# Cross products of split scores: the low part of q padded with zero rows to 128

## Chip, cores, metric

The kernel runs on one core of a Trainium2 chip. The metric is the device time of one execution in microseconds (us); the median over the runs is quoted. A difference of about 0.3% (some 1.1 us) is the least that a measurement of this kernel can tell from none.

## What is computed

One decoder layer on 256 tokens of width 1024, followed by a last RMS normalisation. Cut to its skeleton:

```python
x = x + hybrid_mixer(rmsnorm(x, g_mix), w_in, g_group, sinks, w_out, rel_table)
x = x + memory_cross_attention(rmsnorm(x, g_cross), rmsnorm(mem, g_mem), w_xq, w_xkv, w_xo)
x = x + squared_relu_mlp(rmsnorm(x, g_mlp), w_up, w_down)
return rmsnorm(x, g_final)
```

The mixer has four groups of four heads of width 64: `a` dilated attention, `b` stick-breaking attention, `c` grouped-query attention with a window and sinks, `d` block attention. The cross-attention has four heads of width 64 over 256 memory tokens. In each of the five a block of scores is q k^T with a contraction over 64, in float32:

```python
s = jnp.einsum("bhqe,bhke->bhqk", q, k) * SCALE + bias
```

## The kernel before

**Precision.** Every large product is made of float32r parts. A matrix is split into a high part (ACT rounds it while copying, L313 for weights) and a low part (DVE subtracts, L314). `mm3` (L418 to L422) adds three products: high by high, high by low, low by high. All three contract over 128 rows.

**Work and its order.** Weights stream through SP's queue in halves of 512 KB into 4 `raw` buffers (L299), and are split into 15 `w` buffers (L313, L314). The code records operations in a `Plan` with a price each; `arrange` makes a list schedule of them by the longest way to the end, and the result is one fixed order of instructions for each engine. The order is thus settled before the kernel runs, and each engine works its own queue from front to back. The stages run: loads and normalisation (to about 17 us of the trace), projections of the four groups with the attention of the group before between them (to about 104 us), output projection of the mixer, cross-attention (about 142 to 168 us), MLP, final normalisation.

**Scores.** For the first 128 queries of a mixer group, the scores are plain float32 products over 64 rows (L629). For the second 128 queries of each group, and for both blocks of the cross-attention, they are float32r products made by `stacked` (L597 to L601). `stack_k` puts for each head the high part of k into the head's own 64 rows of `ks`, and the low part into the other 64. `stack_q` puts the high part of q into both halves of `qs`, and the low part into `ql`, 64 rows for each head. So the first product of `stacked` contracts over all 128 rows (high q with both parts of k), the second over the 64 rows of the head (low q with the high part of k). Each has 128 weight columns and 256 moving columns. `attend` calls `stacked` four times for each mixer group, the cross-attention (L782 to L786) four times for each of its two blocks: 24 pairs, 48 products. By the order of PE's instructions the 48 stand in five runs of eight (groups `a`, `b`, `d`, and both blocks of the cross-attention) and two runs of four (group `c`, one run for each half).

**What stands around a run.** In front of it ACT writes `qs` (L592) and DVE writes `ql` (L593). Behind it, in a mixer group, DVE adds the bias and takes the extremum (L665; L649 in group `b`), ACT takes the exponential (L669), PE transposes the weights (L535), DVE or ACT copies them out of PSUM (L242, L243), and PE multiplies by v (L553). In the cross-attention the reduction is L788 and the exponential L793. On POOL stand the memsets of constants and of the ones in v (L345, L477, L358), the reciprocal roots `rstd` (L383), and some DMAs on its own queue.

Of the kernel before, what the change touches and what calls it, by code (L numbers as in the profile page):

```python
# [18 lines left out]
P = 128  # L19
# [23 lines left out]
def _constants():  # L43
    """One-hot of minus the bucket of each distance, and the additive mask of each bias row.
    Column u stands for the distance u - 127. Rows 0-3 dilated, 4-7 window, 8-11 causal, 12 strictly past."""
    d = np.arange(STRIP) - 127
    n = np.maximum(d, 0)
    nf = np.maximum(n, 1).astype(np.float32)
    large = 16 + (np.log(nf / np.float32(16)) / np.float32(math.log(2048 / 16)) * np.float32(16)).astype(np.int32)
    bucket = np.where(n < 16, n, np.minimum(large, 31))  # L50
    onehot = np.zeros((32, STRIP), np.float32)
    cols = np.arange(STRIP)[d >= 0]
    onehot[bucket[cols], cols] = -1.0
    cnt = ((d >= 0) & (d <= 128)).astype(np.int64) + ((d >= 0) & (d % 4 == 0)) + ((d >= 0) & (d % 16 == 0))
    mask = np.zeros((NROW, STRIP), np.float32)
    mask[0:4] = np.where(cnt > 0, -np.log(np.maximum(cnt, 1)), BIG)
    mask[4:8] = np.where((d >= 0) & (d < 128), 0.0, BIG)
    mask[8:12] = np.where(d >= 0, 0.0, BIG)
    mask[12] = np.where(d > 0, 0.0, BIG)
    return onehot, mask  # L60


class Buf:
    """A tile that is taken from its pool when the first operation on it is issued."""

# [20 lines left out]
class Plan:  # L86
    """Records operations with what they read and write, and issues them in the order of a list schedule:
    of the operations that can start when an engine gets free, the one with the longest way to the end."""

# [125 lines left out]
def trunk(ctx: ExitStack, tc: tile.TileContext, a: dict, out: bass.AP):  # L215
# [16 lines left out]

# [1 line left out]
    def act(n, fn, r, w, aps=0):  # L234
# [5 lines left out]
    def copy(n, out_, in_, r, w):  # L240
        """A copy out of PSUM, by whichever engine is free first."""
        plan.add("DVE", 0.065 + n * 1.05e-3, lambda: nc.vector.tensor_copy(out_(), in_()), r, w,  # L242
                 ("ACT", 0.02 + n * 0.00093, lambda: nc.scalar.activation(out_(), in_(), AF.Copy)))  # L243
# [10 lines left out]
    def dma_late(nbytes, fn, r, w):  # L254
        """On the queue of GpSimd."""
        plan.add("POOL", 1.0, fn, r, w)
        plan.add("DMA", max(0.06, nbytes / 360e3), None, [], w)
# [11 lines left out]

# [1 line left out]
    w_in, w_out = a["w_in"][0], a["w_out"][0]  # L271
# [20 lines left out]
    def load(u, *which):  # L292
        """Fetches and splits halves of a unit."""
        n, c = units[u].shape[1] // 2, units[u].shape[2]
        got = parts.setdefault(u, ([], n))[0]
        for part in which or range(2):
            raw = buf("raw", [P, n, c], F32, RAW)
            hi, lo = buf("w", [P, n, c], F32R, SPL), buf("w", [P, n, c], F32R, SPL)
            dma(n * c * 512, lambda raw=raw, part=part: nc.sync.dma_start(raw.t, units[u][:, part * n:(part + 1) * n]), [], [raw])  # L299
            if u == "cq":  # L300
                def view(z, r):
                    return z.t[:, :, tsl(r)].rearrange("p k (g e) -> p k g e", g=2)

                def src(z, r):
                    return z.t.rearrange("p k (g r e) -> p k r g e", g=2, r=2)[:, :, r]

                for r in range(2):
                    act(512, lambda raw=raw, hi=hi, r=r: nc.scalar.activation(view(hi, r), src(raw, r), AF.Copy),
                        [raw], [(hi, r)])
                    dve(512, lambda raw=raw, hi=hi, lo=lo, r=r: nc.vector.tensor_sub(  # L310
                        view(lo, r), src(raw, r), view(hi, r).bitcast(F32)), [raw, (hi, r)], [(lo, r)])
            else:
                act(1024, lambda raw=raw, hi=hi: nc.scalar.activation(hi.t, raw.t, AF.Copy), [raw], [hi])  # L313
                dve(1024, lambda raw=raw, hi=hi, lo=lo: nc.vector.tensor_sub(lo.t, raw.t, hi.t.bitcast(F32)), [raw, hi], [lo])  # L314
            got.append((hi, lo))

    def wt(u, k):
        """Row block k of a unit: the two buffers and the block's place in them."""
        got, n = parts[u]
        return got[k // n], k % n  # L320

# [1 line left out]
    xt = []  # L323
# [36 lines left out]
    def warm_up(n):  # L360
        """Products of nothing, so that the array's clock is up when the first ones come."""
        wps = acct()
# [15 lines left out]

# [1 line left out]
    def rstd_of(ssq, n):  # L380
# [18 lines left out]
    def transpose(dst, src, view, n, keys):  # L399
        """n blocks of 128 columns of view(), transposed side by side into dst."""  # L400
        def go():
# [4 lines left out]
    def gained_T(x, g, hl, t):  # L406
        """The transposed rows of x, times the gain, split: (t, half of the blocks) at a time."""
        tmp = buf("tmp", [P, KB, P], F32, 3)
# [20 lines left out]
    def proj_T(dst, view, u, i, hT):  # L429
        """view()[c, t] = sum_k w[k, c] hT[k, t]"""  # L430
        for k in range(KB):
# [4 lines left out]
    def proj(dst, view, u, hT, t):  # L436
        """view()[t, c] = sum_k hT[k, t] w[k, c]"""
        for k in range(KB):
# [3 lines left out]

# [1 line left out]
    h1 = pair("hT", KB, 2)  # L444
# [15 lines left out]

# [1 line left out]
    bias = {gi: buf("w", [P, 4, S], F32, SPL) for gi in (0, 2, 3)}  # L462
# [7 lines left out]

# [1 line left out]
    def project(gi):  # L472
# [45 lines left out]

# [1 line left out]
    def own(h):  # L520
# [5 lines left out]
    def transpose_probs(w, t):  # L526
        """w [t, 4, s] -> per head the blocks [s, t], each with its buffer."""
        res = []
# [14 lines left out]
    def weigh(pT, v, kv, vkeys):  # L543
        """Weighted values and their sums: [t, 4, 65]."""
        py = pst()
# [24 lines left out]

    # ---- scores of 128 queries and 256 keys by float32r products: a head's two parts of k above each other in the
    #      rows of the array, met by the high part of q twice; then the low part of q with the high part of k ----
    def rows_of(half):
        return slice(half * E, half * E + E)

    def stack_k(k, view, n):
        """Slot 2 i + half: the high part of the head's rows, and in the other rows their low part."""
        ks = buf("ks", [P, 4, S], F32R, 1)
# [7 lines left out]
    def stack_q(q, view):  # L586
        """The high part twice, above each other, and the low part in its own rows."""
        qs, ql = buf("qs", [P, 4, P], F32R, 1), buf("ql", [P, 2, P], F32R, 1)
        for half in range(2):
            own, other, at = rows_of(half), rows_of(1 - half), slice(half, 4, 2)  # L590
            for r in (own, other):
                act(256, lambda r=r, own=own, at=at: nc.scalar.activation(qs[r, at, :], view()[own], AF.Copy), [q], [(qs, half)])  # L592
            dve(256, lambda own=own, at=at: nc.vector.tensor_sub(  # L593
                ql[own, :, :], view()[own], qs[own, at, :].bitcast(F32)), [q, (qs, half)], [(ql, half)])
        return qs, ql

    def stacked(dst, q, i, ks, j):  # L597
        qs, ql = q
        own = rows_of(i % 2)
        nc.tensor.matmul(dst, qs[:, i, :], ks[:, j, :], start=True, stop=False)  # L600
        nc.tensor.matmul(dst, ql[own, i // 2, :], ks[own, j, :], start=False, stop=True)  # L601

# [92 lines left out]
    def rows_mm(acc, hl, u, t, c0, c1, first, last):  # L695
        """acc += columns c0 to c1 of the sum over the two row blocks of a unit"""
        for j in range(2):
# [30 lines left out]

# [1 line left out]
    mT = pair("hT", KB, 2)  # L730
# [4 lines left out]

# [1 line left out]
    pacc = [[acct() for n in range(2)] for t in range(2)]  # L737
# [8 lines left out]

# [1 line left out]
    pk = pst()  # L748
# [8 lines left out]

# [1 line left out]
    def residual(acc, t, r=None):  # L759
# [51 lines left out]
    plan.fixed = MLP_RANK  # L811
# [1 line left out]
    pieces = [[(acct(), 0, 512), (acct(), 512, D)], [(acct(), 0, 512), (acct(), 512, LASTC), (pst(), LASTC, D)]]  # L813
# [3 lines left out]
    def up_rows(i, hid, t):  # L817
        """Two blocks of hidden features for one block of tokens alone."""
        pu = pst()
# [106 lines left out]
```

## Time and profile before

| | us |
|---|---|
| median of three runs | 361.29 |
| lowest, highest run | 360.21, 361.37 |
| span of the profiled execution, first to last instruction | 357.2 |
| PE busy | 347.0 |
| DVE busy | 230.7 |
| ACT busy | 194.1 |
| POOL busy | 24.9 |

The profiled execution's own device time is not listed beside its span; the median of the runs lies 4.1 us above the span, for what is outside the first and the last instruction. PE is TensorE's products, PEld its weight loads, DVE VectorE, ACT ScalarE, POOL GpSimd, SP the engine whose queue issues most DMAs. The start of a product and the start of the next one tell what it holds the array for; the duration that a row prints for a product is longer, since products are pipelined.

### The profile page before, as it was taken

The numbers are of one execution on the slowest core, as the hardware profiler recorded it, in microseconds if no ns is written. First come the engines' busy times: TensorE is split into PE (matmuls) and PEld (weight loads), VectorE is DVE, ScalarE is ACT, GpSimd is POOL, SyncE is SP. The second block draws the span as 40 slices with busy tenths as digits, with TensorE's granted clock in tenths as the row PEclk, the third lists the DMA queues.
The fourth block names the chain that finished last, engine by engine and source line by source line (L and its number), as shares of the span: only waits on it lengthen the run. The fifth ranks groups of instructions, "written<-read, shape, count | busy, mean of one in ns | idle before, by whom it ended". The sixth has DMA issues, their size and how long they took to land.

```text
span 357.2 us, 6139 instructions
## 1 busy us (share of the span) xinstructions
PE 347.0 (97%) x2442; PEld 316.9 (89%) x2442; DVE 230.7 (65%) x370; ACT 194.1 (54%) x313; POOL 24.9 (7%) x44
## 2 busy tenths in 40 slices
PE   7899999999999999999999999999999999999992
PEld 6798999989888889878999999999999999999982
DVE  3857779579886699668946445464555545465254
ACT  6577677377873467684654435354353534535132
POOL 5430100000201005000010000000000000000000
PEclk9999999999999999999999999999999999999998
DMA  8998574640245335825375555655466554653003
GB/s 247 357 348 254 140 217 124 229 119 0 65 167 182 120 118 159 260 65 167 103 252 178 176 163 192 219 181 192 137 218 195 185 200 135 229 190 107 2 0 117
DMA packets 39900, 59.88 MB, mean 168 GB/s; under 512 B 2006, under 2 KB 33040, under 8 KB 39872
## 3 DMA queue, kind: packets, MB, share of 16 engines
q1 hardware_dynamic: 39216, 57.69, 50.3%
q0 software_dynamic: 640, 1.80, 1.7%
q8 instruction: 19, 0.31, 0.3%
q14 instruction: 9, 0.07, 0.1%
q10 hardware_dynamic: 16, 0.00, 0.0%
HBM read 58.42 MB, written 1.07 MB: 167 GB/s over the span
## 4 chain that ended last, share of the span: by engine, by line
PE 91%; DVE 2%; issue 2%; DMA 2%; POOL 1%; ACT 0%; SPq 0%; POOLq 0%; DVEq 0%
PE acc L420 15%; PE acc L421 15%; PE acc L422 15%; PE ps L421 11%; PE ps L420 11%; PE ps L422 11%; PE ps L553 4%; PE ps L403 3%; PE ps L601 2%; PE ps L600 2%; PE ps L535 2%; DMA x<-in_x_dram 2%; POOL rstd L383 1%; PE ps L629 1%; DVE hTlo L397 1%
## 5 line engine op out<-in xcount | busy, mean ns | idle before, releaser
L314 DVE TENSOR_TENSOR w<-raw,w 128x1024 fp32r<-128x1024 f32 x100 | 120.3, 1220 | 83.4 <-ACT w L313 80.0
L313 ACT ACTIVATE w<-raw 128x1024 fp32r<-128x1024 f32 x100 | 103.4, 1054 | 93.7 <-PE ps L421 43.5
L421 PE MATMUL ps<-hTlo,w 128*128 128x256 f32 x256 | 72.2, 282 | 0.0
L420 PE MATMUL ps<-hThi,w 128*128 128x256 f32 x256 | 72.0, 281 | 0.0
L422 PE MATMUL ps<-hThi,w 128*128 128x256 f32 x256 | 71.8, 280 | 0.0
L420 PE MATMUL acc<-w,yThi 128*128 128x512 f32 (+1 forms) x168 | 64.1, 381 | 0.0
L421 PE MATMUL acc<-w,yThi 128*128 128x512 f32 (+1 forms) x168 | 63.0, 375 | 0.0
L422 PE MATMUL acc<-w,yTlo 128*128 128x512 f32 (+1 forms) x168 | 62.5, 372 | 0.0
L422 PEld LDWEIGHTS ps<-hThi,w 128*128 128x128 f32 x256 | 48.4, 189 | 0.0
L420 PEld LDWEIGHTS ps<-hThi,w 128*128 128x128 f32 x256 | 48.2, 188 | 0.1
L421 PEld LDWEIGHTS ps<-hTlo,w 128*128 128x128 f32 x256 | 48.1, 188 | 0.1
L422 PEld LDWEIGHTS acc<-w,yTlo 128*128 128x128 f32 x168 | 31.5, 188 | 6.1
L420 PE MATMUL acc<-hThi,w 128*128 128x256 f32 x128 | 36.6, 286 | 0.0
L420 PEld LDWEIGHTS acc<-w,yThi 128*128 128x128 f32 x168 | 31.6, 188 | 5.7
L421 PEld LDWEIGHTS acc<-w,yThi 128*128 128x128 f32 x168 | 31.7, 189 | 5.2
L421 PE MATMUL acc<-hTlo,w 128*128 128x256 f32 x128 | 36.1, 282 | 0.0
L422 PE MATMUL acc<-hThi,w 128*128 128x256 f32 x128 | 36.0, 281 | 0.0
L383 POOL TENSOR_TENSOR rstd<-var,mhalf 128x1 f32<-128x1 f32 x16 | 14.9, 932 | 149.6 <-DVE var L382 102.8
L420 PEld LDWEIGHTS acc<-hThi,w 128*128 128x128 f32 x128 | 24.1, 188 | 0.5
L422 PEld LDWEIGHTS acc<-hThi,w 128*128 128x128 f32 x128 | 24.2, 189 | 0.1
L421 PEld LDWEIGHTS acc<-hTlo,w 128*128 128x128 f32 x128 | 24.1, 188 | 0.0
L830 ACT ACTIVATE q<-ps 128x512 f32<-128x512 f32 x15 | 9.0, 599 | 11.8 <-PE ps L422 11.8
(151 smaller groups left out, 523.6 us busy)
## 6 DMA issues: line engine op xcount, KB each, us to landing
raw<-in_w_up_dram SPq DMA_DIRECT2D x32, 512.0 KB, 3.8
raw<-in_w_down_dram SPq DMA_DIRECT2D x32, 512.0 KB, 3.8
raw<-in_w_in_dram SPq DMA_DIRECT2D x22, 512.0 KB, 4.9
raw<-in_w_out_dram SPq DMA_DIRECT2D x8, 512.0 KB, 3.4
raw<-in_w_xkv_dram SPq DMA_DIRECT2D x4, 512.0 KB, 3.7
w<-dstrip POOLq DMA_DIRECT2D x3, 512.0 KB, 8.3
x<-in_x_dram SPq DMA_DIRECT2D x2, 512.0 KB, 6.0
tmp<-in_mem_dram SPq DMA_DIRECT2D x2, 512.0 KB, 5.8
```

The lines of the kernel that those rows point to most:

```text
L313: act(1024, lambda raw=raw, hi=hi: nc.scalar.activation(hi.t, raw.t, AF.Copy), [raw], [hi])
L314: dve(1024, lambda raw=raw, hi=hi, lo=lo: nc.vector.tensor_sub(lo.t, raw.t, hi.t.bitcast(F32)), [raw, hi], [lo])
L383: pool(0.5, lambda: nc.gpsimd.tensor_tensor(r.t, v.t, mhalf.t, op=ALU.pow), [v, mhalf], [r])
L403: nc.tensor.transpose(dst[:, tsl(k)], view()[:, tsl(k)], ident.t)
L420: nc.tensor.matmul(dst, lh, rh, start=start, stop=False)
L421: nc.tensor.matmul(dst, lh, rl, start=False, stop=False)
L422: nc.tensor.matmul(dst, ll, rh, start=False, stop=stop)
L535: nc.tensor.transpose(pt[:, tsl(i)], w[:, h, tsl(j)], ident.t)
L553: nc.tensor.matmul(view()[:, h, :], z[:, i, :], v[:, j, kv(h), :], start=j == 0, stop=j == len(pT[h]) - 1)
L600: nc.tensor.matmul(dst, qs[:, i, :], ks[:, j, :], start=True, stop=False)
L601: nc.tensor.matmul(dst, ql[own, i // 2, :], ks[own, j, :], start=False, stop=True)
L830: act(512, lambda: nc.scalar.activation(r.t, pu.t.rearrange("p (i t) -> p i t", i=2), AF.Relu), [pu], [r])
```

## The change

`ql` becomes two buffers of 128 rows and four slots, made once and zeroed by POOL at the start. Calls of `stack_q` take them in turn. The low part of a head goes into its own 64 rows of its own slot; the other 64 rows of the slot stay zero. The second product of `stacked` takes the whole slot and all 128 rows of `ks`, so that the low part of k meets zeros. Comments and docstrings were removed as well.

```diff
     def stack_q(q, view):
-        qs, ql = buf("qs", [P, 4, P], F32R, 1), buf("ql", [P, 2, P], F32R, 1)
+        qs, ql = buf("qs", [P, 4, P], F32R, 1), lows[len(turns) % 2]
+        turns.append(ql)
         for half in range(2):
             own, other, at = rows_of(half), rows_of(1 - half), slice(half, 4, 2)
             for r in (own, other):
                 act(256, lambda r=r, own=own, at=at: nc.scalar.activation(qs[r, at, :], view()[own], AF.Copy), [q], [(qs, half)])
             dve(256, lambda own=own, at=at: nc.vector.tensor_sub(
-                ql[own, :, :], view()[own], qs[own, at, :].bitcast(F32)), [q, (qs, half)], [(ql, half)])
+                ql[own, at, :], view()[own], qs[own, at, :].bitcast(F32)), [q, (qs, half)], [(ql, half)])
         return qs, ql
 
     def stacked(dst, q, i, ks, j):
         qs, ql = q
-        own = rows_of(i % 2)
         nc.tensor.matmul(dst, qs[:, i, :], ks[:, j, :], start=True, stop=False)
-        nc.tensor.matmul(dst, ql[own, i // 2, :], ks[own, j, :], start=False, stop=True)
+        nc.tensor.matmul(dst, ql[:, i, :], ks[:, j, :], start=False, stop=True)
+
+    lows, turns = [buf(f"ql{i}", [P, 4, P], F32R) for i in range(2)], []
+    for z in lows:
+        pool(0.6, lambda z=z: nc.gpsimd.memset(z.t.bitcast(F32), 0.0), [], [z])
```

The order of instructions on PE, DVE, ACT and SP stays as it was, but for line numbers, the name of the tile, and the shape that DVE writes (64x2x128 in place of 64x256). POOL gets two instructions. Its queue near the start, before the change (names are those of the tiles: `mhalf` the exponent for `rstd`, `v` and `vx` the ones in the values, `sink` the sinks):

```order
L345 MEMSET mhalf_119 128x1
L477 MEMSET v_0_121 128x8
L353 DMA sink_123<-in_sinks_dram 128x4
L477 MEMSET v_1_139 128x8
L477 MEMSET v_0_141 128x4
L358 MEMSET vx_146 128x8
L383 TENSOR_TENSOR rstd_161<-var_157,mhalf_119 128x1
```

and with the change:

```order
L345 MEMSET mhalf_119 128x1
L477 MEMSET v_0_121 128x8
L605 MEMSET ql_0_123 128x512
L605 MEMSET ql_0_134 128x512
L353 DMA sink_144<-in_sinks_dram 128x4
L477 MEMSET v_1_153 128x8
L477 MEMSET v_0_157 128x4
L358 MEMSET vx_161 128x8
L383 TENSOR_TENSOR rstd_165<-var_159,mhalf_119 128x1
```

The two memsets stand ahead of the load of the sinks, three small memsets and the first reciprocal root.

## Rows read from the trace of the kernel before

**Rows 1.** Page, part 1: engine, busy us (share of the span), instructions.
```profile
PE 347.0 (97%) x2442; PEld 316.9 (89%) x2442; DVE 230.7 (65%) x370; ACT 194.1 (54%) x313; POOL 24.9 (7%) x44
```

**Rows 2.** Windows: stretch, length, busy us of each engine, PEclk, DMA share, GB/s.
```profile
37.00:71.00 34.00, 34.00 (x293) 33.64 (x293) 25.81 (x48) 20.67 (x36) 1.21 (x3) 1.00 0.60 184
75.00:87.00 12.00, 12.00 (x108) 11.49 (x107) 11.00 (x34) 11.60 (x30) 0.00 (x0) 1.00 0.09 36
...
154.00:162.00 8.00, 7.61 (x51) 6.12 (x51) 5.36 (x9) 5.94 (x10) 0.00 (x0) 1.00 0.22 67
200.00:300.00 100.00, 100.00 (x690) 92.61 (x689) 53.09 (x54) 44.70 (x53) 0.00 (x0) 1.00 0.59 188
```

**Rows 3.** Timeline at 34 us: start, us, engine, line, operation, tiles, shapes.
```profile
34.13 0.36 PE L600 MATMUL ps<-ks,qs 128*128 128x256 f32 x1
34.42 0.38 PE L601 MATMUL ps<-ks,ql 64*128 64x256 f32 x1
...
36.29 0.38 PE L601 MATMUL ps<-ks,ql 64*128 64x256 f32 x1
36.60 1.11 PE L553 MATMUL ps<-v,pT 128*128 128x65 f32 x8
37.52 0.36 PE L420 MATMUL acc<-hThi,w 128*128 128x256 f32 x1
37.72 0.28 PE L421 MATMUL acc<-hTlo,w 128*128 128x256 f32 x1
37.84 0.28 PE L422 MATMUL acc<-hThi,w 128*128 128x256 f32 x1
```

**Rows 4.** Line L601, whole span: duration in ns, first and last start.
```profile
L601 PE MATMUL ps<-ks,ql x24: 378/380/383, 34.4 to 156.4; 64*128 64x256 f32 x24
```

**Rows 5.** Page, part 5: a group of weight loads (busy us, mean ns).
```profile
L422 PEld LDWEIGHTS ps<-hThi,w 128*128 128x128 f32 x256 | 48.4, 189 | 0.0
```

**Rows 6.** Timeline of PE at 146 to 149 us.
```profile
146.13 0.28 PE L422 MATMUL ps<-w,hTlo 128*128 128x256 f32 x1
146.25 0.27 PE L600 MATMUL ps<-ks,qs 128*128 128x256 f32 x1
...
148.64 0.39 PE L420 MATMUL ps<-w,hThi 128*128 128x256 f32 x1
```

**Rows 7.** Timeline at 34.8 us, ACT.
```profile
34.83 0.57 ACT L243 ACTIVATE pT<-ps 128x512 f32<-128x512 f32 x1
```

**Rows 8.** Timeline at 91 to 95 us: ACT's queue and who waits for it.
```profile
91.46 1.29 ACT L581 ACTIVATE ks<-k 64x512 fp32r<-64x512 f32 x2 [0.48 <-PE ps L601]
...
92.77 1.73 ACT L592 ACTIVATE qs<-q 64x256 fp32r<-64x256 f32 x4
...
94.52 0.47 ACT L494 ACTIVATE v<-acc,rstd 128x256 f32<-128x256 f32 x1
...
95.05 0.74 PEld L553 LDWEIGHTS ps<-v,pT 128*128 128x128 f32 x6 [0.17 <-ACT v L494]
```

**Rows 9.** Timeline at 156 to 160 us: softmax of the second cross-attention block.
```profile
156.83 0.69 DVE L788 TENSOR_REDUCE nm<-ps 128x2 f32<-128x512 f32 x1 [0.56 <-PE ps L601]
...
157.55 0.84 ACT L793 ACTIVATE w<-ps,nm 128x256 f32<-128x256 f32 x2 [0.41 <-DVE nm L788]
...
158.11 1.04 PE L535 MATMUL ps<-ident,w 128*128 128x128 f32 x8
```

**Rows 10.** Timeline of POOL, 0 to 8 us.
```profile
0.72 0.20 POOL masks.py:197 MEMSET ident<- 128x128 f32 x1 [0.29 <-POOLq L914]
...
7.56 1.41 POOL L383 TENSOR_TENSOR rstd<-var,mhalf 128x1 f32<-128x1 f32 x1 [3.04 <-DVE var L382]
```

**Rows 11.** Timeline at 49 to 53 us: one weight tile, from split to product.
```profile
49.73 1.06 ACT L313 ACTIVATE w<-raw 128x1024 fp32r<-128x1024 f32 x1 [1.64 <-PE acc L421]
...
51.16 1.22 DVE L314 TENSOR_TENSOR w<-raw,w 128x1024 fp32r<-128x1024 f32 x1
...
52.84 0.28 PE L422 MATMUL acc<-hThi,w 128*128 128x256 f32 x1
```

## The prediction

> **What bounds the kernel now.** I start with the busy times of the engines: PE works 347.0 of the span's 357.2 us [rows 1]. An average hides stages, so the table of stretches comes next. Between 37 and 71 us and through the MLP (200 to 300 us) PE has no idle time at all, while DVE and ACT in the MLP are busy for 53.09 and 44.70 of 100 us [rows 2]. In such stages each microsecond that PE's queue gives up is a microsecond of the kernel. Two places are tighter: from 75 to 87 us DVE is busy for 11.00 and ACT for 11.60 of 12 us, and from 154 to 162 us PE is busy for 7.61 of 8 us, so it already waits a little [rows 2]. There a faster PE may only meet a later operand.
>
> Since busy time of PE includes pipelining, I then read start to start. Products over 128 rows that follow one another start 0.12 us apart: 37.72, 37.84 [rows 3]. The score products, which alternate between 128 and 64 rows, do not: from 34.42 to 36.29 there are six steps in 1.87 us, 0.312 us each, and the step out of the last one, to 36.60, is 0.31 [rows 3]. Both kinds of product have 256 moving columns, so columns do not explain it. The time is lost on both steps, from 128 rows to 64 and from 64 back to 128, with no wait shown at either. I read it as the array having to finish one shape before it starts the other.
>
> **Products of the scores (the one large term).** The line of the second product has 24 products, the first at 34.4 and the last at 156.4 us [rows 4]; with the 24 first products that is 48, in five runs of eight and two of four.
> A run of eight takes 36.60 - 34.13 = 2.47 us behind plain float32 work [rows 3] and 148.64 - 146.25 = 2.39 us behind float32r work [rows 6]. By the same steps a run of four behind float32r work takes 0.20 + 3 x 0.312 = 1.14 us. I count three runs of eight at 2.47 (`a`, `d`, the second cross block), two at 2.39 (`b`, the first cross block) and two of four: 7.41 + 4.78 + 2.28 = 14.47 us.
> With all products over 128 rows, I price a step at 0.12 us, and the first step behind float32 work at 0.20, as from 37.52 to 37.72 [rows 3]. A run of eight is then 0.20 + 7 x 0.12 = 1.04, or 8 x 0.12 = 0.96; a run of four is 0.48. The sum is 3 x 1.04 + 2 x 0.96 + 2 x 0.48 = 6.00 us. PE's queue gives up 14.47 - 6.00 = 8.47 us. The bounds of the step are 0.12 and 0.31; I take 0.12, because the new product has the form of the products that show it: same rows, same columns, same type, accumulating into one tile.
>
> **What is given back to waits.** Three places.
> At 36.60 PE goes on with values weighted by `pT`, which ACT finishes at 34.83 + 0.57 = 35.40 us [rows 7]. The shorter run ends at 34.13 + 1.04 = 35.17, so PE waits until about 35.45: 0.28 us lost.
> Group `c` has both runs of four and so 2 x 0.66 = 1.32 us to give. But the weighted values at 95.05 already wait 0.17 us for `v` from ACT, and ACT gets there by working off 1.29 + 1.73 + 0.47 = 3.49 us almost without a gap from 91.46 to 94.99 [rows 8]. The only idle time in front of that, 0.48 us, is ended by a score product, since `ks` is one buffer. So at most 0.48 of the 1.32 us passes, and DVE, which feeds ACT, was nearly full just before (11.00 of 12 us) [rows 2]. The loss lies between 0.84 and 1.32; I take 1.0.
> In the second cross block the first half's reduction now starts about 0.44 - 0.91 = 0.47 us earlier (its last product is the fourth of the run), the second half's reduction cannot start before that one's 0.69 us are over, and ACT's exponentials follow. Before, the second half's start at 156.83 and 157.55 [rows 9]; now they come about 0.9 us earlier where PE comes 1.43 us earlier. PE's transposes from 158.11 need the first exponential of the second half, ready at 157.55 + 0.42 = 157.97, for the third of them, about 158.33, so 0.36 us are in hand [rows 9]. About 0.55 - 0.36 = 0.19 us is lost, and some tenth more at the copy behind; I take 0.3.
> Sum of losses 0.28 + 1.0 + 0.3 = 1.58 us.
>
> **The small parts.** The two memsets of 128x512 on POOL: one of 128x128 took 0.20 us [rows 10], so four times as much takes at most 4 x 0.20 = 0.8 us each, 1.6 us in all. POOL is idle for 3.04 us before the first reciprocal root at 7.56 [rows 10], and that hides both, with the load of the sinks and the small memsets that move behind them: no cost. The upper bound is the longest gap itself, 3.04 us for each, as other work on POOL could stretch: the gap then hides one, and the other pushes the root and all of POOL behind it by 3.0 us. That is unlikely with a memset of 0.20 us next to it, but it is also what it costs if the cover is gone, and 354.4 + 3.0 = 357.4 us stays inside the range.
> DVE's write of `ql` goes to two strided slots in place of one block, 12 times, 256 elements: I take it unchanged and at no cost, the wait for it being nowhere PE's last one [rows 3, 6]. A second `ql` buffer removes one wait of DVE on earlier products, worth nothing for the same reason. No queue is moved past another.
>
> **Sum.** 8.47 - 1.58 = 6.9 us. The span of 357.2 becomes 350.3 us; with the 4.1 us by which the median of the runs exceeds that span, **354.4 us**. The forecast's own range reaches from 352.8 (nothing lost) to 355.5 us (the losses about twice as large).
>
> **Rivals.**
> *The weights become the pace.* After the first run PE is about 1.15 us ahead. At 52.84 a product uses a low part that DVE finished at 51.16 + 1.22 = 52.38, 0.46 us before [rows 11]. If splits stay where they are, the first two runs' 1.15 + 1.43 us shrink to 0.46, a loss of 2.1 us: 356.5 us. Against it: ACT's split in front of it waited 1.64 us for PE, which frees the buffer [rows 11], so splits move with PE, and the DMA engines are busy for only 0.60 of this stretch [rows 2]. For it: DMA landings need not move as PE does. 0.12.
> *The step does not shrink.* A weight load takes 189 ns [rows 5]; 0.19 + 0.12 is 0.31 us, just the step of the score runs. If that is a load that cannot run beside the product before it, whatever the rows, 48 steps stay 0.31, PE gives up nothing, and the time stays 361.3 us. Against it: the weight loads of 189 ns belong to steps of 0.12 [rows 3, 5], so 128-row loads do run beside 128-row products. 0.06.
> The Trainium skill, page "TensorE: Matmul & The Clock Gate", section "The mechanism", has a rule to this effect: a weight load overlaps products in flight only when its row group differs. By it the sum would be zero and by the rows 8.47 us; the rows decide, and the trace does not agree with the rule for products of 128 rows.
> *Slower, by the clock.* The losses above are new waits of PE. If one of them dropped the granted clock to 1.2 GHz, the work done at that level would take twice as long. This outweighs the 6.9 us and shows as slower from some 8 us of work at the low level on; with 10 us of it in the cross-attention the time is 354.4 + 10 = 364.4 us. For it: nothing but the waits. Against it: the granted clock is 1.00 in every stretch, also from 154 to 162 us where PE is idle for 0.39 us [rows 2], and the new waits are no longer than about 1 us. 0.03.
> The Trainium skill, page "TensorE: Matmul & The Clock Gate", section "Loop structure matters more than you think", warns that waits between bursts of products lower the clock; by it the forecast would move to this rival, and no stretch of this trace shows that.
>
> **How the numbers follow.** Forecast 0.79, weights 0.12, no shrinking 0.06, slower 0.03. Faster by over 0.3% is the forecast and the weights rival: 0.91. Within 0.3% (1.1 us, about what a measurement can tell from no change): 0.06. Slower: 0.03. The range must hold the first two: from 352.4 (nothing lost, and a little for the spread of the runs) to 357.4 us (weights rival, with 0.9 us more).
>
> **What would show it.** Right: in each run the products start 0.12 us apart, a run of eight spans about 1.0 us, and L601's product prints 128 rows; PE goes on at 36.60 with a short wait for `pT`; the wait for `v` near 92 us grows to about 1 us; the MLP begins about 6.9 us earlier and is otherwise the same. Wrong: steps of 0.31 remain; or new waits of products on L314 between 37 and 71 us; or a granted clock under 1.00 before the end; or the first PE wait for `rstd` at 17 us longer than before.

## The result, and the profile after

The changed kernel takes **352.33 us** (median of four runs, 351.41 to 352.86) against 361.33 us for the kernel before in the same comparison: a ratio of 0.974, with a 95% interval of 0.972 to 0.977. That is 9.0 us less. The forecast was 6.9 us less, 354.4 us, and the median lies just below the lower end of the range, 352.4 us. The sign and the place of the gain were right, its size was not. The medians are over all runs, while the ratio and its interval leave out the slow ones (such as one of 366.66 us before), so they need not agree in the last digit.

| | before | changed |
|---|---|---|
| median, us | 361.33 | 352.33 |
| span of the profiled execution, us | 357.2 | 350.9 |
| PE busy, us | 347.0 | 339.3 |
| DVE, ACT, POOL busy, us | 230.7, 194.1, 24.9 | 230.2, 193.8, 25.8 |

The two spans differ by 6.3 us only, the medians by 9.0: a first sign that one profiled execution is not the median one. The changed kernel was therefore profiled twice more, as e2 and e12 below (spans 349.1 and 349.4 us).

Page of the changed kernel, part 1, against [rows 1]:

```profile
PE 339.3 (97%) x2442; PEld 313.8 (89%) x2442; DVE 230.2 (66%) x370; ACT 193.8 (55%) x313; POOL 25.8 (7%) x46
```

PE has the same 2442 products and is busy for 7.7 us less; the other engines do what they did. Timeline of PE in the changed kernel at the first run of eight score products, against [rows 3]:

```profile
35.65 0.35 PE L600 MATMUL ps<-ks,qs 128*128 128x256 f32 x1
35.84 0.27 PE L601 MATMUL ps<-ks,ql 128*128 128x256 f32 x1
35.95 0.28 PE L600 MATMUL ps<-ks,qs 128*128 128x256 f32 x1
...
36.54 0.28 PE L601 MATMUL ps<-ks,ql 128*128 128x256 f32 x1
36.98 1.11 PE L553 MATMUL ps<-v,pT 128*128 128x65 f32 x8 [0.16 <-ACT pT L243]
```

The first step is 0.19 us and the six that follow take 36.54 - 35.84 = 0.70, 0.12 us each, where they were 0.31. The run is over near 36.66 and PE then waits for `pT`, as forecast. Line L601 of the changed kernel over the whole span, against [rows 4]:

```profile
L601 PE MATMUL ps<-ks,ql x24: 274/279/284, 35.8 to 150.7; 128*128 128x256 f32 x24
```

All 24 second products now have 128 rows and last 0.28 us where they lasted 0.38. Timeline of POOL in the changed kernel, against [rows 10]:

```profile
3.74 1.00 POOL L605 MEMSET ql<- 128x512 f32 x2
...
7.67 1.41 POOL L383 TENSOR_TENSOR rstd<-var,mhalf 128x1 f32<-128x1 f32 x1 [2.22 <-DVE var L382]
```

The two buffers are zeroed in 1.00 us inside the gap that was 3.04 us long and still is 2.22; the first reciprocal root comes at 7.67 where it came at 7.56. Windows of the changed kernel after the first run and over the middle of the span, against [rows 2]:

```profile
37.00:70.00 33.00, 33.00 (x281) 32.64 (x282) 25.42 (x49) 20.06 (x37) 1.21 (x3) 1.00 0.64 192
20.00:340.00 320.00, 317.80 (x2296) 294.81 (x2295) 213.46 (x336) 177.88 (x286) 12.49 (x20) 1.00 0.52 165
```

PE is busy for all of the 33 us behind the first run, so the weights did not become the pace, and the granted clock is 1.00, the 2.4 GHz level, from 20 to 340 us.

**Where the time went, place by place.** The execution of e2 (the changed kernel again) has its first score product at 34.14 us and the profiled execution of before at 34.13, so the two can be laid beside each other. Starts of the same products (us) on PE:

| product | before | changed (e2) | ahead by |
|---|---|---|---|
| first of run `a` | 34.13 | 34.14 | -0.01 |
| values behind `a` | 36.60 | 35.23 | 1.37 |
| first of run `b` | 71.69 | 70.37 | 1.32 |
| second product behind `b` (L421) | 74.31 | 71.44 | 2.87 |
| first run of `c`, first product | 87.20 | 84.71 | 2.49 |
| second run of `c`, second product behind | 91.57 | 87.55 | 4.02 |
| values that need `v` | 95.05 | 91.98 | 3.07 |
| first of run `d` | 96.72 | 93.66 | 3.06 |
| first product behind the values that follow `d` (L420) | 100.14 | 95.51 | 4.63 |
| first cross block, first of the run | 146.25 | 141.58 | 4.67 |
| second product behind (L421) | 148.87 | 142.64 | 6.23 |
| second cross block, first of the run | 154.25 | 148.01 | 6.24 |
| transposes behind its values (L535) | 158.11 | 150.31 | 7.80 |
| transposes of its result (L403) | 159.38 | 151.91 | 7.47 |
| last product of the kernel | 350.49 | 342.39 | 8.10 |

The runs give 1.38 (`a`), 1.55 (`b`), 1.53 (`c`, both), 1.57 (`d`) and twice 1.56 us (cross blocks): 9.15 us. Lost again are 0.05 behind `a`, 0.38 ahead of `c`, 0.95 between group `c` and the values that need `v`, and 0.33 in the second cross block: 1.71 us. The other two profiles of the changed kernel, the first one and e12, differ from e2 at `a` alone: there the run and the wait for `pT` take 1.33 and 1.34 us in place of 1.09, and the whole gain up to the last product is 7.85 us. Two of the losses in rows of e2, first ahead of `v` (timeline of ACT and of the weight loads, against [rows 8], and a window):

```profile
91.46 0.47 ACT L494 ACTIVATE v<-acc,rstd 128x256 f32<-128x256 f32 x1
91.50 0.30 PEld L553 LDWEIGHTS ps<-v,pT 128*128 128x128 f32 x2 [0.55 <-DVE nm L669]
91.98 0.74 PEld L553 LDWEIGHTS ps<-v,pT 128*128 128x128 f32 x6 [0.19 <-ACT v L494]
...
87.50:92.00 4.50, 4.09 (x32) 3.46 (x31) 4.37 (x15) 4.27 (x10) 0.55 (x1) 1.00 0.33 120
```

The wait for `v` itself did not grow (0.17 before, 0.19 now); what is new is a wait of 0.55 us of the first load, ended by the maxima `nm` of DVE, which is busy for 4.37 of the 4.50 us there. And in the second cross block (timeline of the weight loads, e2, against [rows 9]):

```profile
150.74 0.64 PEld L535 LDWEIGHTS ps<-ident,w 128*128 128x128 f32 x6 [0.28 <-ACT w L797]
```

The third of the transposes waits 0.28 us for its exponential, as forecast. From there to the last product the changed kernel gains another 0.63 us, with no product changed there. This is taken up at the end.

### The profile page after: what moved, and what is told of

It is laid out like the page before. It is cut to its first block, busy times and chain, and to the rows that moved or that the text cites. A ratio compares the mean times of both kernels' runs of the same rounds, so it can differ in the third digit from the quotient of the medians.

```text
span 350.9 us, 6140 instructions
## 1 busy us (share of the span) xinstructions
PE 339.3 (97%) x2442; PEld 313.8 (89%) x2442; DVE 230.2 (66%) x370; ACT 193.8 (55%) x313; POOL 25.8 (7%) x46
## 4 chain that ended last, share of the span: by engine, by line
PE 79%; DVE 6%; DMA 6%; ACT 4%; issue 2%; SPq 0%; POOLq 0%; POOL 0%; DVEq 0%; ACTq 0%
PE acc L420 13%; PE acc L421 13%; PE acc L422 13%; PE ps L421 11%; PE ps L422 11%; PE ps L420 11%; DMA raw<-in_w_in_dram 4%; PE ps L553 3%; PE ps L403 3%; DMA x<-in_x_dram 2%; DVE w L314 2%; ACT ks L581 1%; PE ps L535 1%; ACT w L673 1%; ACT qs L593 1%
## 5 line engine op out<-in xcount | busy, mean ns | idle before, releaser
L421 PE MATMUL ps<-hTlo,w 128*128 128x256 f32 x256 | 72.0, 281 | 0.0
L420 PE MATMUL ps<-hThi,w 128*128 128x256 f32 x256 | 71.9, 281 | 0.0
L420 PE MATMUL acc<-w,yThi 128*128 128x512 f32 (+1 forms) x168 | 64.1, 381 | 0.0
L421 PE MATMUL acc<-w,yThi 128*128 128x512 f32 (+1 forms) x168 | 62.6, 373 | 0.0
L420 PEld LDWEIGHTS ps<-hThi,w 128*128 128x128 f32 x256 | 48.2, 188 | 0.1
L421 PEld LDWEIGHTS ps<-hTlo,w 128*128 128x128 f32 x256 | 48.1, 188 | 0.1
L420 PE MATMUL acc<-hThi,w 128*128 128x256 f32 x128 | 36.6, 286 | 0.0
L421 PEld LDWEIGHTS acc<-w,yThi 128*128 128x128 f32 x168 | 31.6, 188 | 5.4
L420 PEld LDWEIGHTS acc<-w,yThi 128*128 128x128 f32 x168 | 31.6, 188 | 5.3
L421 PE MATMUL acc<-hTlo,w 128*128 128x256 f32 x128 | 36.1, 282 | 0.0
L420 PEld LDWEIGHTS acc<-hThi,w 128*128 128x128 f32 x128 | 24.1, 188 | 0.4
L421 PEld LDWEIGHTS acc<-hTlo,w 128*128 128x128 f32 x128 | 24.1, 188 | 0.0
```

What stands on the lines that cost most here:

```text
L420: nc.tensor.matmul(dst, lh, rh, start=start, stop=False)
L421: nc.tensor.matmul(dst, lh, rl, start=False, stop=False)
```

## The experiments

Twelve runs follow, three of them (e1, e2, e12) of a kernel without an edit. The letters of the theories are those of the texts that were on record before each run. For each this table splits the profiled execution at three products: the first of run `a`, the first of the first cross block, and the last of the kernel. It takes out what the front part (0 to 34 us) adds from one execution to the next.

| execution | first score product at | to the cross block | from there to the end | first to last | median, us | ratio (95%) |
|---|---|---|---|---|---|---|
| before | 34.13 | 112.12 | 204.24 | 316.36 | 361.33 | |
| e1 before again | 35.32 | 113.71 | 204.26 | 317.97 | 362.23 | 1.000 (0.997 to 1.004) |
| changed | 35.65 | 107.70 | 200.81 | 308.51 | 352.33 | 0.974 (0.972 to 0.977) |
| e2 changed again | 34.14 | 107.44 | 200.81 | 308.25 | 352.97 | 0.976 (0.973 to 0.979) |
| e3 mirrored order | 35.80 | 109.72 | 202.91 | 312.63 | 356.87 | 0.987 (0.984 to 0.990) |
| e4 late zeroing | 38.76 | 106.59 | 200.52 | 307.11 | 354.50 | 0.980 (0.977 to 0.984) |
| e5 zeroing only | 33.67 | 112.12 | 204.25 | 316.37 | 360.80 | 0.998 (0.994 to 1.001) |
| e6 mixer only | 35.93 | 107.47 | 203.60 | 311.07 | 355.85 | 0.979 (0.974 to 0.985) |
| e7 cross only | 33.77 | 113.49 | 200.50 | 313.99 | 358.62 | 0.985 (0.979 to 0.991) |
| e8 all but `d` | 34.24 | 110.58 | 200.79 | 311.37 | 354.82 | 0.977 (0.971 to 0.982) |
| e9 only `d` | 33.60 | 111.86 | 204.09 | 315.95 | 358.15 | 0.988 (0.983 to 0.993) |
| e10 two `ks` | 33.67 | 105.77 | 200.54 | 306.31 | 350.45 | 0.967 (0.963 to 0.971) |
| e11 one low buffer | 35.50 | 106.82 | 200.57 | 307.39 | 351.04 | 0.970 (0.967 to 0.973) |
| e12 changed, beside e11 | 34.12 | 107.69 | 200.82 | 308.51 | 352.21 | 0.973 (0.971 to 0.976) |

Without the fronts, and without the falls of the granted clock that come below, the same kernel repeats to 0.3 us.

**e1: the kernel before once more.** No edit. It asks what lies outside the span, and how the profiled execution of before stands to others.

> The kernel before, unchanged, for its own spread. Theory A (the profiled execution that the sum was made against was a quick one): its executions have spans of 358 to 359.5 us with about 2 us outside the span, 360.2 to 361.4 us in all, and in a new profile the first score product starts 1 to 2 us after 34.13. Theory B (what lies outside the span shrank from 4.1 to 2.0 us with the change): spans again near 357.2 and about 4 us outside.

The profiled execution took 362.06 us with a span of 360.0: 2.06 us lie outside. In every execution listed with both numbers it is 1.8 to 2.1 us, so theory A held for what lies outside; its span, 360.0, lies a little above the 359.5 that A allowed. The prediction's 4.1 us was the sum of 2.1 us outside and some 2 us by which the profiled execution of before was quicker than the median one. Of the 2.8 us between the two spans, 1.2 lie in the front and 1.6 between `a` and the cross block. The windows of e1 show the latter:

```profile
87.00:100.00 13.00, 12.95 (x86) 10.79 (x85) 11.33 (x31) 9.50 (x23) 2.55 (x3) 1.00 0.18 51
101.00:105.00 4.00, 4.00 (x20) 3.60 (x20) 2.92 (x9) 3.00 (x6) 0.00 (x0) 0.57 0.05 18
105.00:150.00 45.00, 45.00 (x291) 39.71 (x288) 36.20 (x59) 28.12 (x47) 6.12 (x7) 1.00 0.51 166
```

For 3.41 us from 101.22 on the granted clock was 0.5, the 1.2 GHz level, and PE had been busy for 12.95 of the 13 us up to 100. The timeline of PE in e1 shows it on the products behind run `d`:

```profile
100.12 0.38 PE L601 MATMUL ps<-ks,ql 64*128 64x256 f32 x1
100.43 1.27 PE L553 MATMUL ps<-v,pT 128*128 128x65 f32 x8
101.46 0.56 PE L420 MATMUL acc<-w,hThi 128*128 128x256 f32 x1
101.82 0.41 PE L421 MATMUL acc<-w,hThi 128*128 128x256 f32 x1
102.04 0.41 PE L422 MATMUL acc<-w,hTlo 128*128 128x256 f32 x1
```

Steps of 0.12 us have become 0.22 (101.82 to 102.04). No wait stands there: the fall came 0.8 us behind the end of a run that alternates between 128 and 64 rows. The profiled execution of before shows no fall until its last product is done.

**e2: the changed kernel once more.** No edit. It asks whether the late first score product of the first profile (35.65) belongs to the change.

> The changed kernel, unchanged, for its own spread beside the others of this list. Theory A: 352 to 353 us, span about 2 us less, and the first score product between 34 and 36 us, differing from run to run. Theory M (the zeroing delays the front by 1.5 us): the first score product at 35.5 us or later in every run.

It does not: the product started at 34.14 here and at 34.12 in e12, so theory M fell. In the first profile the front had been held by a weight tile that landed late, as its timeline shows:

```profile
30.64 1.06 ACT L313 ACTIVATE w<-raw 128x1024 fp32r<-128x1024 f32 x1 [2.00 <-DMA raw<-in_w_in_dram]
...
33.02 0.39 PE L422 MATMUL acc<-hThi,w 128*128 128x256 f32 x1 [0.54 <-DVE w L314]
```

**e3: half of the changes of row count, the 64-row products kept.** On the kernel before, heads 2 and 3 issue their two products the other way round, so that products of the same row count meet.

```diff
-        nc.tensor.matmul(dst, qs[:, i, :], ks[:, j, :], start=True, stop=False)
-        nc.tensor.matmul(dst, ql[own, i // 2, :], ks[own, j, :], start=False, stop=True)
+        two = [(qs[:, i, :], ks[:, j, :]), (ql[own, i // 2, :], ks[own, j, :])]
+        for n, (l, r) in enumerate(two[::1 if i < 2 else -1]):
+            nc.tensor.matmul(dst, l, r, start=n == 0, stop=n == 1)
```

> The kernel before with the second head of each half taking its low product first, so that a half runs 128, 64, 64, 128 rows: the same 48 products and the same queues, 24 changes of the row count in place of 48. Theory C (each change of the row count costs about 0.19 us): steps between two 64-row products and between two 128-row products are 0.12 us, the runs give up 24 x 0.19 = 4.6 us, and the time is about 357 us. Theory D (the 64-row product itself and its load are slow, 0.31 us wherever it stands): 24 steps into and 24 out of 64-row products stay, and the time is 360.5 to 361.5 us.

Timeline of PE in e3, run `a`:

```profile
35.80 0.37 PE L602 MATMUL ps<-ks,qs 128*128 128x256 f32 x1
36.10 0.50 PE L602 MATMUL ps<-ks,ql 64*128 64x256 f32 x2
36.53 0.50 PE L602 MATMUL ps<-ks,qs 128*128 128x256 f32 x2
36.96 0.50 PE L602 MATMUL ps<-ks,ql 64*128 64x256 f32 x2
37.39 0.39 PE L602 MATMUL ps<-ks,qs 128*128 128x256 f32 x1
37.61 1.00 PE L553 MATMUL ps<-v,pT 128*128 128x65 f32 x8
```

A pair of like products takes 0.43 us, 0.12 inside and 0.31 at the change, whichever row count the pair has. The run of eight takes 1.81 us against 2.47, and first to last the kernel gains 3.7 us of the 8.1 (316.36 to 312.63). So what costs is the change of row count, and theory C held: 64-row products that follow one another, here on the same 64 rows, are as fast as 128-row ones. This is the reading that the prediction only argued.

**e4: zeroing moved late.** On the changed kernel the two memsets read `rk`, so that they cannot lie in POOL's gap.

```diff
-        pool(0.6, lambda z=z: nc.gpsimd.memset(z.t.bitcast(F32), 0.0), [], [z])
+        pool(0.6, lambda z=z: nc.gpsimd.memset(z.t.bitcast(F32), 0.0), [rk], [z])
```

> The changed kernel with the two zeroing instructions of POOL behind the second reciprocal root (after 17 us) in place of ahead of the sinks' load. Theory M (zeroing delays the front by 1.5 us): about 350.8 us, first score product at about 34.1 us. Theory N (it is hidden, and what the front takes is set by landings of weights): as the changed kernel within 0.3%, 351.5 to 353 us.

A miss as a test: the added dependency made the list schedule order other work differently too, on PE as well. The first score product came at 38.76, 4.6 us later than in e2, and the rest ran 1.1 us faster. Neither theory can be read from that.

**e5: the zeroed buffers, but the old products.** `stack_q` gets a switch that keeps the block of 64 rows and the 64-row second product; PE, ACT and SP keep the order of the changed kernel. e6 to e9 use the same switch.

```diff
+        if pad:
+            ql = lows[len(turns) % 2]
+            turns.append(ql)
+        else:
+            ql = buf("ql", [P, 2, P], F32R, 1)
...
+        if pad:
+            nc.tensor.matmul(dst, ql[:, i, :], ks[:, j, :], start=False, stop=True)
+        else:
+            own = rows_of(i % 2)
+            nc.tensor.matmul(dst, ql[own, i // 2, :], ks[own, j, :], start=False, stop=True)
```

> The kernel before plus the two zeroing instructions of POOL, whose tiles nobody reads; the second products stay at 64 rows. Theory N (the zeroing is hidden in POOL's idle time): as before within 0.5%, 360 to 362.5 us. Theory M (it delays the front): 1 to 3 us slower.

Timeline of POOL in e5:

```profile
4.43 1.01 POOL L613 MEMSET ql<- 128x512 f32 x2
7.11 1.41 POOL L383 TENSOR_TENSOR rstd<-var,mhalf 128x1 f32<-128x1 f32 x1 [1.67 <-DVE var L382]
```

The ratio 0.998 (0.994 to 1.001) and 316.37 us first to last, as before, say that the zeroing is hidden and gives nothing by itself.

**e6 and e7: mixer only, cross-attention only.** The switch is on for the four head groups and off for the two cross blocks, and the other way round.

> The change in the four mixer groups alone; the cross-attention keeps 64-row second products. By the shifts of the two traces (before, and the changed kernel's second profile) the mixer's runs give up 4.6 us net: 361.3 - 4.6 = 356.7 us. Theory K (part of the gain is that the clock no longer falls behind the runs of the mixer, where a profile of the kernel before shows 3.4 us at 0.5): up to 1.5 us more, about 355.2 us, and no granted clock under 1.00 between 90 and 110 us. Theory L (the falls of the clock have nothing to do with the runs): 356.7 us, and such falls as often as before.

> The change in the cross-attention alone; the mixer keeps 64-row second products. By the shifts of the traces its two runs give up 3.2 us and lose 0.3: 361.3 - 2.9 = 358.4 us. Theory K: the clock still falls behind the mixer's runs in a good part of the executions, mean clock 0.991 or lower in these. Theory L: the mean clocks are those of the changed kernel, mostly 0.996.

e6 gains 6.2 us in the medians and e7 3.4, together 9.6 where the whole change gave 8.3 to 10.2 in its three comparisons. In e6 all of the gain up to the cross block is there (107.47 us), in e7 all of it behind (200.50). e7's stretch in front of the cross block is 1.4 us longer than before's, and a window of e7 shows why:

```profile
99.00:103.00 4.00, 4.00 (x19) 3.60 (x20) 3.32 (x10) 2.74 (x6) 0.00 (x0) 0.57 0.13 53
```

It is the same fall, from 99.48 on, and again right behind run `d`, which alternates in e7. e6, where `d` is padded, shows none there.

**e8 and e9: is it run `d`?** e8 pads everything but `d`, e9 nothing but `d`.

> The changed kernel, but group d's run of eight keeps 64-row second products. Without the clock: 1.5 us more than the changed kernel, 352.5 + 1.5 = 354 us. Theory K (the fall at 101 us belongs to group d's run with its changes of the row count): the fall comes back in part of the executions, which adds up to 1.7 us there, and the median lies at 354 to 355.7 us. Theory L: 354 us, clocks as in the changed kernel.

> The kernel before, with the change in group d's run of eight alone. Without the clock: 1.5 us less, 361.5 - 1.5 = 360 us. Theory K (the fall at 101 us belongs to this run's changes of the row count): no granted clock of 0.5 between 95 and 110 us in the profile, and the median is up to 1.7 us lower still, 358.3 to 359.5 us. Theory L: such falls stay, 360 us.

Window of e8 behind `d`:

```profile
96.00:100.00 4.00, 4.00 (x18) 3.67 (x18) 3.41 (x10) 2.26 (x7) 0.00 (x0) 0.58 0.29 114
```

Windows of e9 behind run `a`, behind `d`, and behind the second cross block:

```profile
37.00:41.00 4.00, 4.00 (x23) 4.00 (x23) 2.29 (x5) 2.49 (x7) 0.55 (x1) 0.57 0.31 85
98.00:104.00 6.00, 6.00 (x49) 5.65 (x48) 5.57 (x17) 5.92 (x12) 0.49 (x1) 1.00 0.37 111
156.00:160.00 4.00, 4.00 (x23) 4.00 (x23) 3.54 (x6) 2.30 (x5) 0.00 (x0) 0.59 0.13 23
```

In e8 the clock fell behind `d` (96.63), the one run left alternating. In e9 it stayed up behind `d` and fell behind `a` (37.23) and behind the second cross block (156.69), which alternate there. So the fall goes with the alternating run, not with the place. The medians point the same way: e8's, 354.82, lies in the range of theory K (354 to 355.7) and e9's, 358.15, just below it (358.3 to 359.5), where theory L had 354 and 360. The fall does not come in every execution: before and e5 alternate everywhere, and e3 at half of the steps, and their profiles show none between 20 and 340 us. Run `d` alone, alternating in e8, costs 311.37 - 308.25 = 3.1 us, of which its own products are 1.57 and the fall about the rest.

**e10: two buffers of stacked `k`, one zeroed buffer.** The gain given back at `v` hangs on ACT, which before had waited for the one `ks` [rows 8]. So `ks` gets a second buffer, and one zeroed buffer pays for its room.

```diff
-        ks = buf("ks", [P, 4, S], F32R, 1)
+        ks = buf("ks", [P, 4, S], F32R, 2)
-        qs, ql = buf("qs", [P, 4, P], F32R, 1), lows[len(turns) % 2]
+        qs, ql = buf("qs", [P, 4, P], F32R, 1), lows[0]
-    lows, turns = [buf(f"ql{i}", [P, 4, P], F32R) for i in range(2)], []
+    lows, turns = [buf(f"ql{i}", [P, 4, P], F32R) for i in range(1)], []
```

> The changed kernel with two buffers for the stacked k and one zeroed buffer for the low part of q, so that ACT and DVE may write the next group's k while PE still reads the last one; the list schedule moves with it. Theory P (the 0.94 us that PE gives back in group c hangs on the single buffer): about 352 us or a little less, and the wait for v behind the two runs of four is under 0.3 us. Theory Q (ACT and DVE are full there anyway): as the changed kernel within 0.4%, or worse where the new order does not fit.

It is the fastest version, 350.45 us, a ratio of 0.967 (0.963 to 0.971), and in group `c` no weight load waits for `v`. But the list schedule also orders other work differently, which e11 and e12 take apart.

**e11 and e12: one zeroed buffer without the second `ks`, and the changed kernel on the same chip.** e11 keeps the last two edits of e10 only.

> The kernel of the two buffers for the stacked k, with that buffer single again: the changed kernel with one zeroed buffer in place of two. Theory P (the second buffer for the stacked k is what gained): as the changed kernel, 352 to 353.5 us, with the wait for v in group c back. Theory R (the other order of the list schedule, or one zeroing less, is what gained): 350 to 351 us.

> The changed kernel beside the one with one zeroed buffer, on the same chip. Theory P: the same within 0.4%. Theory R: some 2 us slower than it. For the clock (theory K): no granted clock under 1.00 between the first 20 us and the last ones in the profile.

e11 is at 351.04 and e12 at 352.21 us. One zeroed buffer is not slower than two; the list schedule gives another order, on PE too, which is 1.1 us shorter first to last than e12's, and here too no load waits for `v`. So a good part of e10's gain is the order, as theory R had it. What the second `ks` adds is not settled: e10 is another 1.1 us shorter first to last in one profile each, but the intervals of e10 and e11 overlap.

## Why the prediction missed

The prediction had the mechanism right. The steps that failed are two terms of its sum, "Products of the scores" and the 4.1 us in "Sum", and it had no term for two smaller gains. From the first score product to the last product the account of e2 is 6.9 forecast, + 0.68 more from the products, - 0.13 for larger losses, + 0.63 behind the cross-attention: 8.1 us. The medians gain another 0.9.

**Step "Products of the scores": 8.47 us, measured 9.15.** The steps inside the runs are 0.12 us, as taken. What the sum left out is the step behind the first product that follows a run. Timeline of PE before, behind run `b`:

```profile
74.08 0.39 PE L420 MATMUL acc<-hThi,w 128*128 128x256 f32 x1
74.31 0.28 PE L421 MATMUL acc<-hTlo,w 128*128 128x256 f32 x1
```

And the same two products in e2:

```profile
71.32 0.28 PE L420 MATMUL acc<-hThi,w 128*128 128x256 f32 x1
71.44 0.29 PE L421 MATMUL acc<-hTlo,w 128*128 128x256 f32 x1
```

It was 0.23 us and is 0.12. The prediction ended each run at the start of that product and so missed 0.11 us per run; over seven runs that is about 0.8 us, against the 0.7 by which the term was short (at `a` the product behind the run is one of the weighted values, whose wait for `pT` is counted in with it). [rows 6] end with such a product, at 148.64; the step behind it was not read.

**Step "Sum": the 4.1 us by which the median exceeds the span.** It was carried over as if it were a constant. Only 2.1 us of it lie outside the span; the other 2 us are what the median execution of before has and its profiled one had not. With 2.05 in its place the sum reads 350.3 + 2.05 = 352.35 us. That this is the measured median is chance: the 0.68 and 0.63 us of the account above are not in that sum, and the profiles of the changed kernel start their first score product anywhere between 34.1 and 35.7.

**What the median had.** First to last, the change gives 316.36 - 308.25 = 8.1 us (7.85 in the other two profiles) between executions without a fall of the clock in that stretch; the medians give 9.0. The rest could be the falls of the clock, which cost 1.6 us in e1 and which came behind no padded run in any profile. How many executions of before have one was not counted: the listings give only the mean clock, which falls at the start lower too. By that mean, 5 of 65 executions of before stand at 0.995 or above, and 8 of 15 of the changed kernel; but the lowest of the changed kernel's is 0.981, below the 0.990 of e2 with its one fall in the front part, so it has falls whose place no profile shows. And the medians of the 5 and the 8, 358.82 and 352.76 us, lie only 6.1 us apart, less than the 8.1: something outside that stretch, most likely the front, must differ between such executions as well. So the cause of the last 0.9 us is argued only, and stays open.

**The clock rival had its mechanism on the wrong side.** It priced a fall that the change might bring by new waits, 364.4 us. Falls do exist here, but between the first score product and the last product they were seen only behind runs that alternate, in stretches in which PE shows no wait, and behind no padded run. The Trainium skill, page "TensorE: Matmul & The Clock Gate", section "Loop structure matters more than you think", which the prediction named there, ties a low clock to waits between bursts; ahead of e1's fall the trace shows no such wait (12.95 busy us of 13). That is weak evidence against it, since a busy time adds up printed durations and can't show whether the array stood still inside the steps of 0.31 us.

**What was given back: 1.58 us forecast, 1.71 measured,** but spread differently. At `a` 2.47 - 1.04 - 0.28 = 1.15 us net was forecast: 1.14 came in the first profile and in e12, 1.38 in e2, where PE goes on with the values 1.09 us after the first score product. In `c` 1.0 was forecast and 0.38 + 0.95 = 1.33 came, and ahead of the values it was DVE's maxima rather than `v` that ended the longer wait; the sign named for it, a wait for `v` of about 1 us, did not come (0.19). The second cross block lost 0.33 where 0.3 was forecast (the working there writes 0.44 - 0.91 for 0.91 - 0.44; the size, 0.47, is right).

**The small parts were right.** Two memsets took 1.00 us (bound 1.6) inside the gap, and e5 shows that they cost nothing.

**The other rivals fell.** "The step does not shrink" fell by the steps of 0.12. "The weights become the pace" fell by 33.00 busy us of 33 and by the lead, which in e2 is still 1.32 us at run `b`, of 1.37 behind `a`.

## What to carry to other kernels

Where PE is the bound, read start to start: a change between products of 64 and of 128 rows cost 0.19 us beyond the step of 0.12 here, in either direction, so either pad with zeros that are written once, or put products of equal row count side by side (half of the changes gave half of the gain). Before a sum is built on one profiled execution, set its own time beside its span and look where it stands among the runs; what the median has beyond it may be the very thing that the change removes. And take a gain behind a list schedule as the sum of the edit and of the order that it happens to bring, until a run has held one of them still.

## What was not expected of the hardware

**The clock falls behind alternating runs.** In four profiles the granted clock went to 0.5 for 3.4 us between the first score product and the last product: at 101.22 (e1), 99.48 (e7), 96.63 (e8), 37.23 and 156.69 (e9). Each time a run that changes row count had ended 0.4 to 1.1 us before, and PE showed no wait in it; none was seen behind a padded run. Such runs are not the only thing that stands ahead of a fall: the clock went down for 3.4 us in the front part too, at 7.82 (e2), 8.27 (e5), 7.32 (e7) and 7.88 (e8), long before any score product, and e2 is the changed kernel. PE and a window of e2:

```profile
7.93 1.33 PE L403 MATMUL ps<-ident,x 128*128 128x128 f32 x5 [1.99 <-DMA x<-in_x_dram]
...
7.82:11.23 3.41, 3.30 (x13) 2.65 (x14) 2.27 (x5) 2.42 (x6) 0.00 (x0) 0.50 1.05 254
```

In these four the fall came within 0.3 us of the end of a wait of PE for `x`, 1.40 to 1.99 us long; in the ten profiles without a fall there that wait is 0.26 to 1.17 us. The Trainium skill, page "TensorEngine Tiling (Array Packing)", section "Key Properties", says that changing the tiling mode drains the array; the steps of 0.31 us agree with that. That the clock can fall behind such stretches, these runs show; why some executions keep it, they don't.

**The MLP runs 0.3% faster with the same products.** From 205 to 345 us of before, laid against the same products of the others, the lead changes steadily, at the same granted clock of 1.00:

```
change of the lead over before, 205 to 345 us
before again (e1) 0.00, zeroing only (e5) -0.01, mirrored (e3) 0.00
changed, e2, e12 0.48 each; mixer only 0.48; all but d 0.48
only d 0.71; cross only 0.64; two ks 0.56; one low buffer 0.56
late zeroing (e4) 1.32
```

It repeats to 0.01 us for one kernel on different executions. In e2 most of it lies between products of 256 columns, whose mean step is 0.1182 us before and 0.1176 in e2; in e7 and e9 that step is no shorter (0.1185 and 0.1184), and the gain lies between products of 512 columns (0.2300 us in both, 0.2335 before). Every kernel with a padded product has it and none without. With the stretch from the cross-attention to 205 us it is 0.6 us of the 8.1 in e2; no term of the prediction had it, and no run here was made to find its cause.
